# Moving 28 of 32 output stores of a streaming softmax mixture to the second hardware DMA queue

## The chip, the cores and the metric

The kernel runs on one core of one Trainium2 chip. The metric is the device time of one execution, in microseconds (us). Every timed run quoted here was fast, at a granted clock of 1.0, so all of them may be compared.

A word on names. VectorE is DVE in the profile, ScalarE is ACT, and SP is SyncE, which does nothing here but issue DMAs. "q1" is the DMA queue that SP issues to (the first hardware queue) and "q10" the one that ScalarE issues to (the second). A "row" below is one DMA descriptor that carries data: one contiguous run of bytes of one partition. The trace keeps a record of each (start, duration, size, queue), but not the number of the engine.

## The reference, cut to what matters

```python
# logits [32, 128, 4, 4096] f32, prior [32, 128, 4] f32 -> out [32, 128, 4096] f32
prior_probs = softmax(prior, axis=-1)
softmax     = exp(logits - max) / sum(exp(logits - max))     # over 4096
mixture     = sum(prior_probs[..., None] * softmax, axis=2)  # over the 4 heads
```

A batch reads 8.4 MB and writes 2.1 MB. All in all 335.55 MB must pass between HBM and SBUF, so this is a streaming kernel.

## The kernel before

A batch is loaded as one DMA (128 partitions of 64 KB each) into one of two `ltile` buffers. ScalarE takes the exponential of each head and its sum, VectorE scales and adds the heads into one of two `acc` buffers, and `acc` is stored (128 rows of 16 KB). Loads and stores all go through SP, so they are worked off in one order.

```python
    lpool = ...tile_pool(name="lpool", bufs=2)   # loads, 64 KB per partition each
    epool = ...tile_pool(name="epool", bufs=2)   # exponentials
    apool = ...tile_pool(name="apool", bufs=2)   # acc
    def pieces(b):
        return 1 if b >= B - 3 else H            # heads in one load DMA
    def load(b):
        lt = lpool.tile([P, H, V], FP32, name="ltile")
        n = pieces(b)
        for h in range(0, H, n):
            nc.sync.dma_start(out=lt[:, h : h + n], in_=logits[b, :, h : h + n, :])
    def store(b, lo=0, hi=V):
        nc.sync.dma_start(out=out[b, :, lo:hi], in_=accs[b][:, lo:hi])
    # ... prior softmax, load(0), load(1) ...
    for b in range(B):
        # ... accs[b] = a tile of apool (the load's own buffer for the last two) ...
        for h in range(H):
            nc.scalar.activation(et, lt[:, h], AF.Exp, accum_out=dsum)       # L98
            # coeff = prior / dsum                                            L101, L102
            # h == 0: acc  = et * coeff                                       L104
            # else:   acc += et * coeff                                       L106
            # the last head of the last batch goes in chunks, stored in two halves
        if b + 2 < B:
            load(b + 2)
        if b < B - 4:
            store(b)
        elif b == B - 3:          # stores 28, 29 behind the last load
            store(b - 1); store(b)
        elif b == B - 2:
            store(b)
```

The softmax here doesn't subtract the row's maximum and nothing guards it: scores larger than these inputs give would overflow.

## Time and profile before

| | before |
|---|---|
| median of 3 runs | 786.32 us (786.19 to 786.34) |
| share of the 16 DMA engines' time, q1 | 99.6% |
| VectorE busy, ScalarE busy | 70%, 60% |
| store: issue to landing | 31.3 us |
| VectorE's wait for a free acc | 24.9 us in all |

The first fence has lines from the page of the kernel before. The DMA line is the busy share of the DMA engines in 40 equal slices, in tenths. The q lines give rows and semaphore writes, MB, and share of 16 engines' time. The L104 line gives, after the bars, busy us and ns of one, then the idle time just before and what ended it. The last two give the number of issues, KB each, and us from issue to landing.

```profile
span 783.5 us, 1004 instructions
...
DMA  9999999999999999999999999999999999999998
...
q1 hardware_dynamic: 10656, 335.55, 99.6%
q10 hardware_dynamic: 48, 0.07, 0.0%
...
L104 DVE TENSOR_SCALAR acc<-etile,coeff 128x4096 f32<-128x4096 f32 x30 | 70.6, 2353 | 24.9 <-DMA out_dram<-acc 24.9
...
out_dram<-acc SPq DMA_DIRECT2D x30, 2048.0 KB, 31.3
...
ltile<-in_logits_dram SPq DMA_DIRECT2D x29, 32.2
```

The reader should see that one queue fills the engines in every slice, and that VectorE's wait for a free acc is small against the span.

The second fence is the timeline of the kernel before over one steady period (start us, duration us, engine, line, what; idle time before and its releaser in brackets). "SPq" lines are DMA issues.

```profile
280.61 0.34 SPq L51 DMA_DIRECT2D out_dram<-acc  x1
283.01 3.62 ACT L98 ACTIVATE etile<-ltile 128x4096 f32<-128x4096 f32 x1 [8.20 <-DMA ltile<-in_logits_dram]
...
287.88 2.35 DVE L104 TENSOR_SCALAR acc<-etile,coeff 128x4096 f32<-128x4096 f32 x1 [0.77 <-DMA out_dram<-acc]
...
299.06 0.33 SPq L45 DMA_DIRECT2D ltile<-in_logits_dram  x1
...
304.83 0.34 SPq L51 DMA_DIRECT2D out_dram<-acc  x1
307.31 3.62 ACT L98 ACTIVATE etile<-ltile 128x4096 f32<-128x4096 f32 x1 [8.28 <-DMA ltile<-in_logits_dram]
```

Two consecutive first exponentials, at 283.01 and 307.31, are one period apart, 24.3 us. The next load is issued at 299.06, as soon as ScalarE has read the last head of the batch whose buffer it takes. The load before it lands only at 307.3. So there are 8.3 us in which the next load is already queued.

The records of the rows complete this: a 64 KB row takes 2418 ns (27.1 GB/s on each of 16 engines, 433.6 GB/s in all), a 16 KB row 611 ns. Each engine has 8 of each per batch, which makes 24.2 us: the period. The Trainium skill ("DMA: Bandwidth & Descriptors", section Where 436 GB/s comes from) puts the ceiling of the ports into SBUF at 435.2 GB/s, one of several limits that it lists; the 64 KB rows agree with this one, 0.4% below it.

### The profile page before, as it was taken

Reading aid. Unit: us, or ns where it says so; the run is one execution under the profiler, and the core shown is the slowest. Engines: PE = TensorE matmul, PEld = TensorE weight load, DVE = VectorE, ACT = ScalarE, POOL = GpSimd, SP = SyncE. Lnnn points to the kernel's source line nnn. Section 1 sums busy time; section 2 is a strip of 40 time slices with the busy share of each in tenths; the row PEclk is TensorE's granted clock in tenths of the full one; section 3 lists DMA queues with packets and bytes.
Section 4 is the critical chain, followed back from the end, with each engine's and each line's share of the span. In section 5 each row is a group of like instructions: output and inputs, shape, how many; then the busy total and the mean of one; then the engine's idle time right before and its main releaser. Section 6 shows DMA issues by size and latency. Waiting matters only on the chain.

```text
span 783.5 us, 1004 instructions
## 1 busy us (share of the span) xinstructions
DVE 547.2 (70%) x408; ACT 472.7 (60%) x258; POOL 0.2 (0%) x4
## 2 busy tenths in 40 slices
DVE  3587568766687666786667866668766687666995
ACT  0776554765547755567555675555765557755881
POOL 0000000000000000000000000000000000000000
DMA  9999999999999999999999999999999999999998
GB/s 385 458 405 415 428 435 417 460 432 435 428 407 449 428 428 432 441 426 458 432 428 421 428 443 428 432 442 417 464 432 432 428 412 445 432 421 432 431 428 343
DMA packets 10712, 335.68 MB, mean 428 GB/s; under 512 B 1200, under 2 KB 1200, under 8 KB 1232
## 3 DMA queue, kind: packets, MB, share of 16 engines
q1 hardware_dynamic: 10656, 335.55, 99.6%
q10 hardware_dynamic: 48, 0.07, 0.0%
q14 instruction: 8, 0.07, 0.0%
HBM read 268.50 MB, written 67.11 MB: 428 GB/s over the span
## 4 chain that ended last, share of the span: by engine, by line
DMA 62%; DVE 18%; ACT 12%; issue 6%; DVEq 0%; ACTq 0%; SPq 0%
DMA ltile<-in_logits_dram 55%; ACT etile L98 12%; DVE acc L106 12%; DMA out_dram<-acc 8%; DVE ltile L106 3%; DVE coeff L102 1%; DVE acc L104 1%; DVE ltile L104 1%; DVE rden L101 1%; DVE ltile L112 0%; DVEq L152 0%; ACTq L98 0%; SPq L45 0%; DVEq L104 0%
## 5 line engine op out<-in xcount | busy, mean ns | idle before, releaser
L98 ACT ACTIVATE etile<-ltile 128x4096 f32<-128x4096 f32 x120 | 433.5, 3613 | 279.4 <-DMA ltile<-in_logits_dram 232.4
L106 DVE SCALAR_TENSOR_TENSOR acc<-etile,coeff,acc 128x4096 f32<-128x4096 f32 x90 | 403.6, 4484 | 3.2
L101 DVE RECIPROCAL rden<-dsum 128x1 f32<-128x1 f32 x128 | 20.4, 160 | 182.4 <-ACT etile L98 179.8
L104 DVE TENSOR_SCALAR acc<-etile,coeff 128x4096 f32<-128x4096 f32 x30 | 70.6, 2353 | 24.9 <-DMA out_dram<-acc 24.9
L98 ACT ACTIVATE ltile<-ltile 128x4096 f32<-128x4096 f32 x8 | 28.8, 3607 | 3.0 <-DMA ltile<-in_logits_dram 3.0
L102 DVE TENSOR_TENSOR coeff<-rden,pp 128x1 f32<-128x1 f32 x128 | 20.4, 160 | 4.4
L106 DVE SCALAR_TENSOR_TENSOR ltile<-ltile,coeff 128x4096 f32<-128x4096 f32 x5 | 22.4, 4484 | 0.2
L98 ACT ACTIVATION_READ_ACCUMULATOR etile<-ltile 128x1 f32 x120 | 22.4, 186 | 0.0
L60 DVE TENSOR_REDUCE pmax<-pr 32x128 f32<-32x512 f32 x1 | 0.7, 675 | 11.1 <-DMA pr<-in_prior_dram 11.1
L64 ACT ACTIVATE pe<-pc 32x512 f32<-32x512 f32 x1 | 0.6, 629 | 10.0 <-DVE pc L62 10.0
L112 DVE SCALAR_TENSOR_TENSOR ltile<-ltile,coeff 128x1024 f32<-128x1024 f32 x4 | 4.9, 1278 | 0.0
L104 DVE TENSOR_SCALAR ltile<-ltile,coeff 128x4096 f32<-128x4096 f32 x2 | 4.7, 2353 | 0.1
L64 ACT ACT_TABLE_LOAD x1 | 1.3, 1283 | 1.2 <-PEq L141 1.2
L78 DVE STREAM_TRANSPOSE pp<-pn 32x32 f32<-32x32 f32 x16 | 1.9, 170 | 0.1
L98 ACT ACTIVATION_READ_ACCUMULATOR ltile<-ltile 128x1 f32 x8 | 1.5, 186 | 0.0
L66 DVE TENSOR_REDUCE psum<-pe 32x128 f32<-32x512 f32 x1 | 0.7, 674 | 0.7 <-ACT pe L64 0.7
L71 DVE TENSOR_TENSOR pn<-pe,prec 32x512 f32<-32x512 f32 x1 | 1.0, 1020 | 0.0
L68 DVE RECIPROCAL prec<-psum 32x128 f32<-32x128 f32 x1 | 0.9, 942 | 0.0
L62 DVE TENSOR_TENSOR pc<-pr,pmax 32x512 f32<-32x512 f32 x1 | 0.7, 678 | 0.0
L141 POOL MEMSET const-bfloat16-1.0<- 128x1 bf16 x1 | 0.1, 101 | 0.0
L141 POOL MEMSET const-uint8-127<- 128x1 uint8 x1 | 0.1, 101 | 0.0
L141 POOL MEMSET const-float32-0.0<- 128x1 f32 x1 | 0.1, 98 | 0.2 <-issue 0.2
(1 smaller groups left out, 0.1 us busy)
## 6 DMA issues: line engine op xcount, KB each, us to landing
out_dram<-acc SPq DMA_DIRECT2D x30, 2048.0 KB, 31.3
ltile<-in_logits_dram SPq DMA_DIRECT2D x12, 2048.0 KB, 22.6
out_dram<-ltile SPq DMA_DIRECT2D x1, 2048.0 KB, 20.6
out_dram<-ltile SPq DMA_DIRECT2D x2, 1024.0 KB, 8.1
ltile<-in_logits_dram SPq DMA_DIRECT2D x29, 32.2
pr<-in_prior_dram ACTq DMA_DIRECT2D x1, 64.0 KB, 10.3
```

Of the source, the lines that this page charges most:

```text
L60: nc.vector.reduce_max(pmax, pr, axis=AX.X)
L62: nc.vector.tensor_sub(pc, pr, pmax.unsqueeze(2).to_broadcast([B, S, H]))
L64: nc.scalar.activation(pe, pc, AF.Exp)
L68: nc.vector.reciprocal(prec, psum)
L71: nc.vector.tensor_mul(pn.rearrange("b h s -> b s h"), pe, prec.unsqueeze(2).to_broadcast([B, S, H]))
L78: nc.vector.transpose(pp[32 * t : 32 * (t + 1), h, :], pn[:, h, 32 * t : 32 * (t + 1)])
L98: nc.scalar.activation(et, lt[:, h], AF.Exp, accum_out=dsum)
L101: nc.vector.reciprocal(rden, dsum)
L102: nc.vector.tensor_mul(coeff, rden, pp[:, h, b : b + 1])
L104: nc.vector.tensor_scalar_mul(out=acc, in0=et, scalar1=coeff)
L106: nc.vector.scalar_tensor_tensor(out=acc, in0=et, scalar=coeff, in1=acc, op0=ALU.mult, op1=ALU.add)
L112: nc.vector.scalar_tensor_tensor(out=acc[:, cs], in0=et[:, cs], scalar=coeff, in1=acc[:, cs], op0=ALU.mult, op1=ALU.add,)
```

## The change

Its intent is that a store need not stand behind the load that was issued before it. The last four stores stay where they were, behind the last load.

```diff
-    def store(b, lo=0, hi=V):
-        nc.sync.dma_start(out=out[b, :, lo:hi], in_=accs[b][:, lo:hi])
+    def store(b, lo=0, hi=V, eng=nc.sync):
+        eng.dma_start(out=out[b, :, lo:hi], in_=accs[b][:, lo:hi])
@@ for b in range(B):
+        if 0 < b < B - 3:
+            store(b - 1, eng=nc.scalar)
@@
         if b + 2 < B:
             load(b + 2)
-        if b < B - 4:
-            store(b)
-        elif b == B - 3:
+        if b == B - 3:
             store(b - 1)
             store(b)
```

## The prediction

> What bounds the kernel now. The DMA engines. The page's queue list gives the one data queue 99.6% of the 16 engines' time; VectorE is busy 70%, ScalarE 60%. 335.55 MB must move whatever the order, at 428 GB/s. The trace's packet records show each engine taking one descriptor after the other without gaps: 2418 ns for a 64 KB load row (27.1 GB/s), 611 ns for a 16 KB store row (26.8 GB/s). A batch costs an engine 8 x 2418 + 8 x 611 ns = 24.2 us; the timeline shows that period (first exponentials at 283.01, 307.31, 331.56).
>
> Is the queue ever empty? No. In the timeline a load is issued 16.0 us after the first exponential of the batch whose buffer it takes (283.01 to 299.06); the load before it lands 24.3 us after that point: some 8 us spare. At the end the last stores lie back to back; the engines run out only in the last 4 us.
>
> What the change does. It adds and removes no byte and no descriptor. It moves 28 store issues (0.35 us each on SP's queue; the one issue on ScalarE's took 0.42 us) to ScalarE, 12 us in all, inside its 279 us of waits. By the built order, stores 0 and 1 stand before the first exponential of the next batch, so ScalarE waits there for VectorE (batch 0 ends at 44.9, the data is there at 42.57: about 2.8 us with the issue); later ones stand after that exponential, when VectorE has been done for 2.5 us (304.8 against 307.3). Both are smaller than the loads' lead.
>
> What it moves in the engines. Now a store waits behind the load issued before it (31.3 us from issue to landing). The Trainium skill ("DMA: Bandwidth & Descriptors", Queues, rings and completion order) says that an engine alternates between queues packet by packet; the trace agrees: the prior's 2 KB rows on the second queue went one by one between 64 KB rows, 84 ns each. So one 16 KB row per 64 KB row: the store spreads over one load and lands 24 to 27 us after issue. The load is stretched to 24.2 us, which is the period anyway. VectorE's wait for a free acc (24.9 us in all) shrinks or stays; it doesn't bound. The same page (Issuing engines are not separate DMA queues) says that a second queue saves issue time alone; SP's is off the critical path.
>
> A cost that could appear: switching. In the prior's case the first switch was free, and the 64 KB row after the second took about 92 ns longer on each engine. Once per store that is 28 x 0.09 = 2.6 us; per pair of rows 28 x 8 x 0.09 = 20 us. A gain that could: the 9 ns or so that a row costs above its size, at most 4 us.
>
> Prediction: 786.5 us, range 783 to 792. Faster by over 2%: 0.03; within 2%: 0.90; slower: 0.07.
>
> Right if: both queues together fill about 99.5%, the second with 58.7 MB; the period between first exponentials stays at 24.2 to 24.4 us; 64 KB rows stay near 2418 ns; stores land some 25 us after issue, loads still about 32.
>
> Wrong if: rows take longer when queues alternate or loads and stores mix (the period grows, rows or gaps show it); or an engine overlaps a load with a store (rows of both queues running at once, over 435 GB/s); or later loads starve the queue (DMA share under 98%).

## The result, and the profile after

The changed kernel took 784.78 us (median of 4 runs, 784.57 to 785.19) against 786.33 us for the kernel before (4 runs, 786.19 to 787.5). The ratio is 0.9978, with a 95% interval of 0.996 to 0.9995. Ratios here are the mean time of one kernel's fast runs over that of the other's fast runs of the same rounds, so they are not quite the ratio of the medians quoted. A gain of 0.2% is clear of the noise.

The same lines of the page after (the first operation on acc is line L106 now):

```profile
span 782.8 us, 977 instructions
...
DMA  9999999999999999999999999999999999999997
...
q1 hardware_dynamic: 6624, 276.83, 82.0%
q10 hardware_dynamic: 4080, 58.79, 17.5%
...
L106 DVE TENSOR_SCALAR acc<-etile,coeff 128x4096 f32<-128x4096 f32 x30 | 70.6, 2353 | 50.1 <-DMA out_dram<-acc 50.0
...
out_dram<-acc ACTq DMA_DIRECT2D x28, 2048.0 KB, 30.0
...
ltile<-in_logits_dram SPq DMA_DIRECT2D x29, 31.3
```

The two queues together fill 99.5% of the engines, as the one did. But a store still takes 30.0 us to land, not 24 to 27, and VectorE's wait for a free acc has doubled, from 24.9 to 50.0 us. Neither costs anything that can be told (loads_halved, below, tests it). The timeline after, over one period:

```profile
285.52 3.62 ACT L100 ACTIVATE etile<-ltile 128x4096 f32<-128x4096 f32 x1 [7.21 <-DMA ltile<-in_logits_dram]
285.63 0.34 ACTq L51 DMA_DIRECT2D out_dram<-acc  x1
...
291.52 2.35 DVE L106 TENSOR_SCALAR acc<-etile,coeff 128x4096 f32<-128x4096 f32 x1 [1.90 <-DMA out_dram<-acc]
...
302.49 0.33 SPq L45 DMA_DIRECT2D ltile<-in_logits_dram  x1
...
309.70 3.62 ACT L100 ACTIVATE etile<-ltile 128x4096 f32<-128x4096 f32 x1 [7.24 <-DMA ltile<-in_logits_dram]
309.81 0.34 ACTq L51 DMA_DIRECT2D out_dram<-acc  x1
```

The period is still 24.2 us (285.52 to 309.70). The store is issued by ScalarE's queue right behind the first exponential. VectorE waits 1.90 us for the store of two batches before, whose acc it needs. The load is issued at 302.49 and the load before it lands at 309.7: the lead has shrunk from 8.3 to 7.2 us, and it is enough. The windows view of two such periods (stretch, length, busy us of DVE, ACT and POOL with instruction counts, clock, DMA share, GB/s) shows full engines. It counts a row whole in the stretch in which the row starts, so a share can come out a little over 1.00:

```profile
285.50:309.70 24.20, 16.83 (x12) 14.73 (x8) 0.00 (x0) 1.00 1.00 433
309.70:333.90 24.20, 16.83 (x12) 14.74 (x9) 0.00 (x0) 1.00 1.00 434
```

Why 30 us? The records of one engine tell (put together by matching each row's start to the end of the one before; L is a load row, S a store row, and a bar marks the semaphore write that ends a DMA on that engine; the time is us from the span's start):

```
286.09 S (the store before)   286.70 L   289.11 | of that store   289.12 L
291.53 S   292.14 L   294.55 S   295.16 L   297.57 S   298.18 L   300.60 S   301.20 L
303.62 S   304.22 L   306.64 S   307.25 | of the load   307.25 S   307.86 L
310.27 S   310.88 L   313.29 | of this store
```

The engine takes one row from each queue in turn. The semaphore write is a turn as well. So a store of 8 rows and a semaphore needs 9 turns, and so does a load. The store issued at 285.63 first waits for the 9th turn of the store before it, then takes its own 9, each behind a turn of the load queue, which is 2.4 us for a row. The second queue is therefore always just behind: it never empties in this steady state. That is the part of the change that matters, and the experiments below push it off balance.

### The profile page after: what moved, and what is told of

It reads as the page before. It is cut to its first block, busy times and chain, and to the rows that moved or that the text cites. A ratio compares the mean times of both kernels' runs of the same rounds, so it can differ in the third digit from the quotient of the medians.

```text
span 782.8 us, 977 instructions
## 1 busy us (share of the span) xinstructions
DVE 544.9 (70%) x408; ACT 472.7 (60%) x258; POOL 0.2 (0%) x4
## 3 DMA queue, kind: packets, MB, share of 16 engines
q10 hardware_dynamic: 4080, 58.79, 17.5%
## 4 chain that ended last, share of the span: by engine, by line
DMA 73%; DVE 18%; ACT 6%; issue 1%; DVEq 0%; ACTq 0%
DMA ltile<-in_logits_dram 39%; DMA out_dram<-acc 34%; DVE acc L108 10%; ACT etile L100 6%; DVE ltile L108 3%; DVE acc L106 3%; DVE ltile L106 1%; DVE coeff L104 1%; DVE ltile L114 0%; DVE rden L103 0%; DVEq L152 0%; ACTq L100 0%; ACTq L51 0%; DVEq L106 0%
## 5 line engine op out<-in xcount | busy, mean ns | idle before, releaser
L103 DVE RECIPROCAL rden<-dsum 128x1 f32<-128x1 f32 x128 | 20.2, 158 | 156.3 <-ACT etile L100 156.3
L106 DVE TENSOR_SCALAR acc<-etile,coeff 128x4096 f32<-128x4096 f32 x30 | 70.6, 2353 | 50.1 <-DMA out_dram<-acc 50.0
L106 DVE TENSOR_SCALAR ltile<-ltile,coeff 128x4096 f32<-128x4096 f32 x2 | 4.7, 2353 | 0.1
## 6 DMA issues: line engine op xcount, KB each, us to landing
ltile<-in_logits_dram SPq DMA_DIRECT2D x29, 31.3
```

Of the source, the lines that this page charges most:

```text
L103: nc.vector.reciprocal(rden, dsum)
L106: nc.vector.tensor_scalar_mul(out=acc, in0=et, scalar1=coeff)
```

## The experiments

Each kernel ran on one chip beside runs of the kernel before; not every experiment had the same chip, so ratios are compared across experiments. "Stretched" below is the sum over all rows of their duration above the usual one of their size (2418, 1213, 611, 309 ns for 64, 32, 16, 8 KB), divided by 16 engines. "End" is the time in the last 30 us or so in which engines have no row left, averaged over 16, with the 1.2 to 1.9 us after the last row left out. Both come from the records of the profiled run.

### The two kernels again

The edit is none, in both cases.

> The kernel before, unchanged, as a measure of the noise: ratio 1.000, within 0.999 to 1.001, some 786.3 us. Its packet records should again hold about 3.3 us (summed over rows, over 16 engines) of row time above 2418 and 611 ns; if they hold 2.1 us as the changed kernel's do, the difference in stretched rows between the two profiles is chance.

> The changed kernel, unchanged, against five rounds of before. Theory 1, the gain of 0.2% is real and comes from fewer stretched 64 KB rows: 784.6 to 785.2 us, ratio 0.998, stretched row time again near 2.1 us. Rival, the gain is chance: the interval holds 1.000.

The kernel before against itself gave 0.9994 (0.9982 to 1.0007), so the noise is about 0.1%. The changed kernel gave 0.9971 (0.9958 to 0.9985), median 784.62 us. A third time, it gave 0.9976:

> The changed kernel once more beside late14_fixed: 784.6 to 785.2 us, ratio 0.997 to 0.998, stretched rows near 2.0 us, idle at the end near 2.8 us.

It measured 784.82 us, 0.9976 (0.9964 to 0.9988). The gain of 0.2 to 0.3% is real.

```
                span     stretched   end
before          783.46     3.32      2.22
before_again    785.40     2.96      4.52
after           782.79     2.14      2.72
after_again     782.84     1.90      2.93
after_third     783.10     2.14      3.01
```

In all three profiles of the changed kernel about 1 us less of row time is stretched than in the two of the kernel before. Its end varies less, but two profiles of the kernel before are few to say so, and one of them ends more evenly than any of the changed kernel. With the time before the first row and the small overlaps of the records these columns account for each span within 0.01 us, so the whole difference lies in them. Why rows stretch is not told by this, but where is: from 80 to 320 us of the span the stretched time is 0.84 and 1.02 us in the kernel before and 0.05 us in each profile of the changed kernel. In the first 80 us it is 1.5 to 2.1 us in both.

### Stores in halves: first queue, then second

The store of batches 0 to 27 is cut in two DMAs of 8 KB rows, in the kernel before (halves_first) and in the changed one (halves_second):

```diff
-            store(b - 1, eng=nc.scalar)
+            store(b - 1, 0, V // 2, eng=nc.scalar)
+            store(b - 1, V // 2, V, eng=nc.scalar)
```

> Control for the next run: stores of 0 to 27 cut in two halves (8 KB rows), all still on the first queue. In one queue, rows go in order, so the store lands about 31 us after issue as before, with some 3 us at most for 28 x 8 more rows at 7 ns or so each and the semaphores: 786 to 789 us.

> The same halves on the second queue. Theory 1, the engine takes one descriptor of each queue in turn, whatever its size: a store of 16 rows and 2 semaphores needs 18 turns while a load has 9, so the stores fall behind the loads; the second half lands 40 us or more after issue, VectorE's wait for a free acc grows well over the 50 us of the changed kernel (to 100 us or more), and the time moves little (785 to 790 us), because whichever queue has rows left keeps the engines busy. Rival, the engine shares by bytes or by DMA: the store lands after about 30 us as with 16 KB rows, and the wait for acc stays near 50 us.

In the first queue the halves cost nothing that can be told: 787.35 us, ratio 1.0002 (0.9988 to 1.0016), 29.8 us from issue to landing. In the second queue the same halves cost 16%: **911.01 us**, ratio 1.158 (1.1538 to 1.1621). Turn taking was foreseen and the wait for acc grew as said, but "the time moves little" was wrong by far. The DMA line of the page and two lines of the waits view (engine, line, waited for: us in total, times, longest) of halves_second:

```profile
DMA  9999996987969969699697896996969979699999
```

```profile
ACT etile L101 <- DVE rden L104: 247.4, 42, 18.5
DVE acc L107 <- DMA out_dram<-acc: 240.3, 14, 19.2
```

VectorE now waits 240.3 us for stores, in 14 stalls of up to 19 us, and the DMA engines, full before, have holes. The timeline of one hole:

```profile
291.99 3.62 ACT L101 ACTIVATE etile<-ltile 128x4096 f32<-128x4096 f32 x1 [5.35 <-DMA ltile<-in_logits_dram]
292.44 0.83 ACTq L51 DMA_DIRECT2D out_dram<-acc  x2
...
315.15 2.35 DVE L107 TENSOR_SCALAR acc<-etile,coeff 128x4096 f32<-128x4096 f32 x1 [19.06 <-DMA out_dram<-acc]
...
322.38 3.62 ACT L101 ACTIVATE etile<-ltile 128x4096 f32<-128x4096 f32 x1 [1.08 <-DVE rden L104]
...
326.12 0.33 SPq L45 DMA_DIRECT2D ltile<-in_logits_dram  x1
```

And the windows view of the same stretch (columns as above; the last two are the DMA share and GB/s):

```profile
292.00:315.00 23.00, 0.73 (x3) 7.30 (x4) 0.00 (x0) 1.00 0.95 403
315.00:319.60 4.60, 4.38 (x4) 2.00 (x1) 0.00 (x0) 1.00 0.76 319
319.60:327.10 7.50, 7.43 (x5) 5.42 (x4) 0.00 (x0) 1.00 0.13 44
327.10:337.00 9.90, 7.69 (x9) 7.92 (x5) 0.00 (x0) 1.00 0.95 392
```

Read together: a store of 16 rows and 2 semaphores needs 18 turns, and a load offers 9. The store pair issued at 273.33 had only its first half through by 299, and the second half landed at 315.03. VectorE got its acc at 315.15, ScalarE could go on at 317.6, and read the last head of the batch at 322.38, so that the next load was issued at 326.12. The load in flight had ended by then (its last semaphore writes are at 312.5 to 314.1). What was left in the second queue ran out at 319.6, and then all 16 engines stood still for 7.5 us, until the new load's first rows at 327.1. (The 0.13 in that stretch is these rows: some start just before 327.10 and are counted there whole.) I had argued beforehand that whichever queue has rows left keeps the engines busy. That holds only while one has. A starved store holds back the next load by the chain acc, VectorE, exponentials, `ltile`, which here takes 11 us from 315.15 to 326.12, more than the work still queued.

The records account for the loss against the changed kernel's profile: 122.6 us more of span, of which 103.0 us are missing rows in mid-run (89.8 us with all engines idle, in 12 holes of about 7.5 us), 20.2 us stretched rows (some 8 us of it in the first rows after a hole, which take 2.4 to 3.6 us instead of 2.418, and some 10 us in the last row of each load on its engine; why is not shown), and 1.8 us for more, smaller rows; the end and the overlaps take 2.4 us off again.

### Loads in halves too, and loads alone

Both of these change the loads of the kernel with its stores on the second queue, in both_halved on top of halves_second, in loads_halved with whole stores:

```diff
     def pieces(b):
-        return 1 if b >= B - 3 else H
+        return 1 if b >= B - 3 else H // 2
```

> Stores as in halves_second (two halves of 8 KB rows on the second queue), and the loads cut in two as well (32 KB rows), so a batch has 18 turns in each queue again. Theory 1, what cost 125 us was the count of turns, 18 against 9: the stall goes, the engines are never idle together in mid-run, the store pair lands about 30 us after issue, 786 to 791 us (some 4 us of row overhead: 16 more rows a batch at 7 to 9 ns). Rival, small store rows or two store issues on ScalarE's queue cost it: still far over 800 us.

> The changed kernel with only the loads cut in two (32 KB rows): 18 turns for a load, 9 for a store. Theory 1: the store is through after about half a load and lands 18 to 22 us after issue instead of 30, VectorE's wait for acc falls from 50 us to under 5; the time does not gain, since that wait bounds nothing: 785 to 788 us (8 more rows of load a batch cost about 2 us in all). Rival, the wait for acc still costs something in the changed kernel: under 784 us.

With 18 turns on each side, both_halved took 787.09 us, ratio 1.0007 (0.9993 to 1.002): the 16% are gone, although the store rows and the two issues on ScalarE's queue are those of halves_second. No moment in mid-run has all engines idle, and the second half of a store lands 31.3 us after its issue, where in halves_second it took 41 us every second time. This is what the count of turns says. The edit does one thing more: ScalarE can start when half a load is there. No run separates the two in their effect on the time. Its waits view adds something that I had not expected:

```profile
DVE acc L107 <- DMA out_dram<-acc: 135.3, 27, 5.4
```

VectorE waits 135.3 us for stores in this kernel, 27 times, 5.4 us at most, and that is free too. The wait alone is not the cost; the 19 us were, because they outlasted the queued work.

In loads_halved (18 turns for a load, 9 for a store) the store lands in 18.4 us and the wait for it is gone; two lines of its page:

```profile
L106 DVE TENSOR_SCALAR acc<-etile,coeff 128x4096 f32<-128x4096 f32 x30 | 70.6, 2353 | 1.4 <-DVE coeff L104 0.3
...
out_dram<-acc ACTq DMA_DIRECT2D x28, 2048.0 KB, 18.4
```

Its time is 786.48 us, ratio 1.0001 (0.9985 to 1.0016). It has 2.1 us more of nominal row time (rows at their usual durations) than the changed kernel, as was estimated, and by the medians it is 1.7 us slower. So the 50 us of wait in the changed kernel were worth some 0.4 us at most by this, which is within the noise.

### The last four stores on the second queue as well

```diff
-            store(b - 1)
-            store(b)
+            store(b - 1, eng=nc.scalar)
+            store(b, eng=nc.scalar)
```

(the stores of batches 30 and 31 likewise)

> All stores on the second queue, the last four too. Theory: stores 28 and 29 then take turns with the last load, whose rows are 16 KB as well, so the last load lands later by up to their 9.7 us, the last head is computed later and the final halves find idle engines: 788 to 796 us, and the engines stand idle for some us near the end. Rival, the order at the end does not matter either, as the bytes are the same: 784 to 786 us.

It took 792.66 us, ratio 1.0081 (1.0067 to 1.0095), as expected. The windows of the end, first of all_second, then of the changed kernel:

```profile
735.00:762.00 27.00, 20.62 (x15) 15.98 (x10) 0.00 (x0) 1.00 1.01 431
762.00:772.00 10.00, 7.20 (x5) 6.83 (x3) 0.00 (x0) 1.00 1.01 431
772.00:782.00 10.00, 5.66 (x6) 4.30 (x4) 0.00 (x0) 1.00 0.15 66
782.00:792.00 10.00, 4.34 (x4) 0.00 (x0) 0.00 (x0) 1.00 0.51 211
```

```profile
735.00:762.00 27.00, 26.48 (x22) 22.25 (x13) 0.00 (x0) 1.00 1.00 428
762.00:772.00 10.00, 9.46 (x7) 3.39 (x2) 0.00 (x0) 1.00 1.02 435
772.00:783.00 11.00, 0.00 (x0) 0.00 (x0) 0.00 (x0) 1.00 0.58 247
```

In all_second the early stores take turns with the last load, whose rows are now of the same 16 KB. VectorE and ScalarE get their heads later (VectorE is busy 20.62 us of the stretch from 735 to 762 instead of 26.48) and work on until 781 (ScalarE) and 786 (VectorE), while the engines have nothing to move (DMA share 0.15) and then must still write the end. In the changed kernel the compute is done by 772, and the stores kept back fill the engines. Keeping the last four stores behind the last load is worth about 8 us here.

### Half of the stores on the second queue

To find where the 0.2 to 0.3% come from, only stores 0 to 13 (early14) or only stores 14 to 27 (late14) go through the second queue:

```diff
-            store(b - 1, eng=nc.scalar)
+            if b - 1 < 14:                      # late14: b - 1 >= 14
+                store(b - 1, eng=nc.scalar)
@@ ... the other stores after load(b + 2), on SP, as before
```

> Stores 0 to 13 on the second queue, 14 to 27 on the first as before. If the gain of 0.2 to 0.3% comes from fewer stretched 64 KB rows, which stand in the first 320 us of the profiles of before: the whole gain stays, 784.6 to 785.3 us, row time above nominal near 2.0 us. If it comes from the second half or the end: 786 us or more.

> Stores 14 to 27 on the second queue, 0 to 13 on the first: the other half of early14 (786.2 us). If the stretched rows of the first 320 us are what the changed kernel saves, this one keeps them (3.0 to 3.3 us above nominal) and gains nothing: 786.2 to 787 us, ratio 0.999 to 1.001. If the gain comes from how evenly the 16 engines end, it may keep it: 784.6 to 785.5 us with under 3 us of engine idle time at the end.

early14 took 786.18 us, 0.9995 (0.9983 to 1.0008), so it does not keep the whole gain, as I had expected of one theory; its stretched time (2.72 us) and its end (3.30 us) are in between.

late14 took 797.81 us, 1.0137 (1.0116 to 1.0157), which neither theory had. Two lines of its timeline and one of its windows:

```profile
377.72 0.37 ACTq L51 DMA_DIRECT2D out_dram<-acc  x1
...
406.01 2.35 DVE L107 TENSOR_SCALAR acc<-etile,coeff 128x4096 f32<-128x4096 f32 x1 [21.83 <-DMA out_dram<-acc]
```

```profile
406.00:418.00 12.00, 11.85 (x8) 7.42 (x4) 0.00 (x0) 1.00 0.11 39
```

The DMA engines stand almost still for 12 us, once. The built program shows why: at the batch where the stores change queues, the pool gave batch 15 the same acc buffer as batch 14 (they have one address in the build; in the other kernels the two buffers alternate). VectorE then waited 21.83 us for store 14, which had been issued at 377.72, and the load queue ran dry as in halves_second. late14_fixed names the two buffers apart:

```diff
-    apool = ...tile_pool(name="apool", bufs=2)
+    apool = ...tile_pool(name="apool", bufs=1)
-            accs[b] = apool.tile([P, V], FP32, name="acc")
+            accs[b] = apool.tile([P, V], FP32, name=f"acc{b % 2}")
```

> late14 again, with the two acc buffers named apart, so that the build can no longer give batch 15 the buffer of batch 14 (in late14 it did, and VectorE waited 21.8 us there for store 14). If that one shared buffer cost the 11 us: no stretch with all engines idle in mid-run, 785 to 787 us. If the switch of queues itself did: still 795 us or more. For the gain: with the stretched rows of the first 320 us kept, 786.0 to 786.8 us; if the gain sits at the end, 784.6 to 785.3 us.

It took 787.02 us, 0.9996 (0.9982 to 1.0011), with no hole. So the shared buffer had cost the 11 us, and late14 says nothing of the gain. late14_fixed has 3.43 us stretched and an end of 3.97 us: like the kernel before, and no faster.

Each half alone gives no gain that can be told from noise; the whole gives 0.2 to 0.3%. The records do show that the queue of the stores matters for the stretching. From 80 to 320 us it is 0.7 to 1.0 us in each of the five profiles with the stores of that stretch on the first queue, and 0.05 to 0.14 us in each of the seven with them on the second, halves_second with its holes left aside. But that does not make the gain by itself: early14 has this part and is no faster, and before_again has less stretched time than before and took longer. What stretches some 64 KB rows, why fewer of them when loads and stores alternate, and where the gain comes from, stay open.

None of the variants beats the changed kernel. At these row durations it is near its floor: of its 782.8 us of span, 777.0 are rows at their usual durations, and what is left is the start, the stretching and the uneven end, less 2.5 us of overlap.

## Why the prediction was right

- **The bound.** Right. It said that the engines' own row rate bounds, and that the period would stay at 24.2 to 24.4 us: it is 24.2. Both queues together were to fill about 99.5%, the second with 58.7 MB; they fill 82.0% + 17.5%, and q10 moved 58.79 MB. 784.78 us lies in the range of 783 to 792; the centre was 1.7 us too high. Part of this was luck: VectorE's wait grew where it was said to shrink, and that stayed free because the loads still had a lead of 7.2 us, a margin that the prediction had not held against later stores.
- **Turn by turn.** Right, and it is the core of the matter. The Trainium skill ("DMA: Bandwidth & Descriptors", Queues, rings and completion order) says that an engine goes round its queues packet by packet; in this trace a turn is one row, of 64 or of 16 KB alike, and halves_second against both_halved shows that turns, not bytes, are shared out.
- **"lands 24 to 27 us after issue".** Wrong in size: 30.0 us. The sum left out two terms that the records show: the wait for the store before it on the same queue (from 285.63 to 291.53 on the engine shown), and the turn of the semaphore write, which stands behind one more load row of 2.4 us.
- **"VectorE's wait for a free acc shrinks or stays".** Wrong: it doubled to 50.0 us. With a landing at 24 to 27 us it would have shrunk; by the same two terms it did not. The store is now issued 0.1 us after the next batch's first exponential (285.63 against 285.52), where it was issued 2.4 us before it (280.61 against 283.01). Being 2.5 us later and landing only some 1.4 us sooner after the issue, it frees acc about 1.1 us later in each period: the wait went from 0.77 to 1.90 us. "It doesn't bound" was right: loads_halved has 1.4 us of that wait and is no faster, both_halved has 135.3 us and is no slower.
- **Cost of switching.** Neither of its sizes (2.6 or 20 us) is seen: 64 KB rows stay at 2418 ns in the median, and the stretched time is lower than before. The gain of "at most 4 us" from the 9 ns that a row costs above its size did not come either, as each size of row keeps its duration; the gain that there is, 1.5 to 2.4 us by the medians, was not forecast by any step. Rows are stretched 0.8 to 1.0 us less between 80 and 320 us, but early14 has that without the gain, so where the gain comes from stays open.
- **The loads' lead.** Right: it holds. But it was called "some 8 us spare" as if that were safe, and nothing in the prediction asked what happens once stores fall behind. halves_second shows that the same queue assignment with 8 KB store rows loses 16%.

## What to carry to other kernels

In these runs, where two DMA queues both had work, each engine took one row of each in turn, whatever its size (8 to 64 KB), so compare turns, not bytes: rows plus semaphore writes per iteration on either queue. If the queue with the smaller rows has more turns per iteration than the other, its DMAs can fall behind as in halves_second, and the loss appears not on that queue but where the buffers it frees hold back the next load. Where one queue already fills the engines, a second one has next to nothing to give: look first whether the engines are ever idle, and leave stores that only delay the last load behind it.

## What the Trainium skill lacked or had wrong

- "DMA: Bandwidth & Descriptors", Queues, rings and completion order, says that an engine drains a whole packet, typically 9 to 17 descriptors, of one queue before it switches. That typical size does not hold here: the engine switched after every single descriptor, 64 KB or 16 KB (the rule itself holds if each of these is a packet of its own, which the trace does not tell), and the semaphore write took a turn of its own (one store: 8 rows and 1 semaphore, in 9 turns between load rows).
- The same page (Issuing engines are not separate DMA queues, and the rule against spreading DMAs for bandwidth) says that issuing from several engines only saves issue time. With balanced turns that holds (ratio 0.997 to 0.998), but the page does not warn of the loss when turns are uneven: 911.01 against 787.35 us for the same DMAs on one queue.
- The same page, Why small descriptors are slow, gives a fixed overhead of about 3 cycles per packet. Here rows of 64, 32, 16 and 8 KB took 2418, 1213, 611 and 309 ns: some 8 ns above a rate of 27.2 GB/s (an estimate from the first two durations), whichever queue they came from. At the page's 850 MHz that is an estimated 7 cycles; the page names descriptor metadata as a second overhead, and no run splits the 8 ns, so this shows more than the 3 cycles in all, not that they are wrong.
- No page that I read tells that the first rows after the engines have been idle take longer: 2.4 to 3.6 us for 64 KB rows in halves_second, instead of 2.418 us. Whether it is the idleness that does it is not shown, as the last rows of loads took longer there too, without a hole before them.
